# Regrouping the sixteen row blocks of h in a hybrid decoder block

## The chip, the core and the metric

The kernel runs on one core of one Trainium2 chip. The metric is the device time of one execution in microseconds (us), the median of several runs. A change of 0.2% is 1.6 us.

## The reference, cut to what matters

One decoder sub-layer for 256 tokens of width 2048, in float32. A conditioning vector `c` gives shift, scale and gate; `x` is normalised and modulated into `h`, and one wide product with `w_in` (2048 x 11824) feeds everything behind it.

```python
ada = c @ w_ada + b_ada
shift, scale, gate = jnp.split(ada, 3, axis=-1)
h = rms_norm(x, g_pre) * (1.0 + scale[:, None, :]) + shift[:, None, :]
proj = h @ w_in
(qa, kc, vc, ks, vs, kw, vw, ga, za, qb, kb, vb, zb, ma, mb) = jnp.split(proj, IN_SPLITS, axis=-1)
...
oa = nsa_attention(qa, kc, vc, ks, vs, kw, vw, ga, ...)
ya = (oa * jax.nn.silu(za)) @ w_br_a
ob = dilated_mixture(partial_rope(qb), partial_rope(kb), vb)
yb = (ob * jax.nn.silu(zb)) @ w_br_b
merged = jax.nn.sigmoid(ma) * ya + jax.nn.sigmoid(mb) * yb
out = merged @ w_out
return x + gate[:, None, :] * rms_norm(out, g_post)
```

A row block below is 128 of the 2048 rows of `w_in`, and with it 128 of the columns of `h`; there are sixteen, 0 to 15. A row block of `h` can be made only when the 2 x 128 entries of `ada` that belong to it (its shift and its scale) have been summed over all of `c`, and for one block that takes two 1 MB pieces of `w_ada`.

## The kernel before, in words

**Products.** The columns of `w_in` are cut into panels of 512 (one of 256, `kw`, and one of 304, `vw`): kc, ks, two of qa, kw, vw, two each of qb, kb, vb, za, zb, and four each of ma and mb. A weight item (`w_item`, L440) is one load of up to 1024 columns by 128 rows of float32: two row blocks of one panel, or one row block of two neighbouring panels. Each item is loaded into one of six `raw` buffers (`dma`, L552), split by ScalarE into a rounded part `wH` (L583) and by VectorE into the rest `wL` (L584), each with three buffers; then TensorE multiplies it for both halves of the 256 tokens: wH with the rounded h (L648), wH with the rest of h (L650), wL with the rounded h (L653). Two row blocks of a 512-column panel are 12 such products. For za and zb the operands are swapped (L638, L640, L643), and the same item is 24 products of half the size.

**Passes.** Since h comes block by block, the panels are gone over in passes (`PASSES`, L27): block 0; blocks 1 and 2; blocks 3 to 6; blocks 7 to 15. At the end of its pass, a panel's partial sum is moved out of PSUM and added to what lies in SBUF (`evac`, L727: L748 on ScalarE, L750 and L752 on VectorE). Between the third and the fourth pass lies a stretch called `FILL`: there only za and zb go on, with blocks 7 to 12. Their sums stay in the eight PSUM banks from the third pass to the end of `FILL`, where the four panels finish one after the other. The four panels of ma start late: their blocks 0 to 2 are put at the end of the second pass, and their sums stay in PSUM until they have had their blocks of the third.

**h.** The pieces of `w_ada` are ada items. Each is a load of 1 MB (128 x 2048, one row block of one half of `ada`), which VectorE multiplies by `c` and sums in one instruction (L595). Of the first twelve, six go into a tile `early`; the others, and all later ones, share a ring of two buffers, `raw_ada` (`RAW_ADA` = 2). `PIECES` (L32) says which blocks of h are made together and in which pass their ada items run; `spread` (L453) deals them out between the weight items of the pass, over the first `frac` of them, after `skip` items. After the last ada item of a group, `make_h` (L302) makes the group: two small VectorE instructions (L305, L306), one ScalarE instruction for each block (L311), the rounding on ScalarE (L318), and the rest on VectorE (L320). A product that needs a block of a group waits for that whole group (`need`, L695).

**Order.** The list of items is the order in which the program is written. Loads are issued seven items ahead (`LOADS`) from the one queue of SyncE, which works in order: a load that waits for its buffer holds up all loads behind it. Splits and ada sums are written three items ahead (`AHEAD`). On each engine the tile framework then fixes an order when the program is built, by place in the list and by when it expects operands. TensorE takes the items in the order of the list. Attention and the rest (`side_main`) are written as steps, one step for each weight item of the last pass.

Of the kernel before, what the change touches and what calls it, by code (L numbers as in the profile page):

```python
# [23 lines left out]
THETA = 500000.0  # L24
C_QA, C_KC, C_KS, C_KW, C_ZA, C_QB, C_KB, C_VB, C_ZB, C_MA, C_MB = (
    0, 1024, 1536, 2048, 2608, 3632, 4656, 5680, 6704, 7728, 9776)
PASSES = ((0, 1), (1, 3), (3, 7), (7, 16))  # L27
FILL = (7, 13)
KEPT = ("za", "zb")
LATER = ("ma",)  # L30
SECOND = ("kc0", "qa0", "kw0", "vw0", "qa512", "qb0", "ks0", "qb512", "kb0", "kb512", "vb0", "vb512")
PIECES = (((1, 3),), ((3, 7),), ((7, 10), (10, 13)), ((13, 16),))  # L32
AHEAD = 3
RAW = 6
RAW_ADA = 2
# [21 lines left out]
def _build(ctx, tc, d_in, out):  # L57
# [216 lines left out]
    xH = big.tile([128, KT, S], F32R, name="xH")  # L274
# [17 lines left out]
    xL, xT = Parts(), {}  # L292
# [123 lines left out]
    items = []  # L416
# [23 lines left out]
    def w_item(w, kt0, nk, c0, jobs):  # L440
        it = Item()
        it.kind, it.kt0, it.nk, it.jobs, it.whole = "w", kt0, nk, jobs, False
        it.n = sum(j.n for j in jobs)
        it.src = weights(w, kt0, nk, c0, it.n)
        return it

    def w_part(w, a, b, c0, job):
        return [w_item(w, kt, min(2, b - kt), c0, [job]) for kt in range(a, b, 2)]

    def w_job(w, a, b, c0, n, srcT, key):  # L450
        return w_part(w, a, b, c0, Job(n, a, b, srcT, key))

    def spread(ws, others, frac, skip=0):  # L453
        res, j = [], 0
        for i, w in enumerate(ws):
            res.append(w)
            want = max(0, min(len(others), math.ceil(len(others) * (i + 1 - skip) / (frac * (len(ws) - skip)))))
            res.extend(others[j:want])
            j = want
        res.extend(others[j:])  # L460
        return res
# [15 lines left out]
    def pieces(i):  # L477
        return [it for p in PIECES[i] for it in ada_items(p)]

    a, b = PASSES[0]  # L480
    ws = []
    soon = [p for p in partial if p[0] not in LATER]
# [9 lines left out]
    for n, it in enumerate(ws):  # L492
        items.append(it)
        if n in SUM_BEHIND:
# [3 lines left out]
    a, b = PASSES[1]  # L498
# [1 line left out]
    ws += [it for p in seconds for it in w_job("w_in", a, b, p[1], p[2], (xH, xL), ("proj", 1, 0, p))]  # L500
    pass1 = len(items)
    late_jobs = [(p, Job(p[2], 0, PASSES[2][1], (xH, xL), ("proj", 0, 0, p))) for p in partial if p[0] in LATER]
    ws += [it for p, job in late_jobs for it in w_part("w_in", 0, b, p[1], job)]
    items += spread(ws, pieces(1), 0.8, 3)
    a, b = PASSES[2]
    kept_jobs = [(p, Job(p[2], a, FILL[1], (xH, xL), ("proj", 2, 0, p))) for p in soon if p[0] in KEPT]
    ws = [it for p, job in late_jobs for it in w_part("w_in", a, b, p[1], job)]
    ws += [it for p in soon if p[0] not in KEPT
           for it in w_job("w_in", a, b, p[1], p[2], (xH, xL), ("proj", 2, 0, p))]
    ws += [it for p, job in kept_jobs for it in w_part("w_in", a, b, p[1], job)]  # L510
    items += spread(ws, pieces(2), 0.9, 2)
    ws = [it for p, job in kept_jobs for it in w_part("w_in", *FILL, p[1], job)]
    items += spread(ws, pieces(3), 0.8)
    a, b = PASSES[3]
    pass3 = len(items)
    for n, p in enumerate(panels):
        a_ = FILL[1] if p[0] in KEPT else 0 if p[0] == "mb" else a
        ws, cks = w_job("w_in", a_, b, p[1], p[2], (xH, xL), ("proj", 3, 1, p)), []
        if n in (3, 4):
            for q in range(4):  # L520
                it = Item()
                it.kind, it.which, it.q, it.nk, it.n = "ck", n - 3, q, 4, 256
                it.src = weights(("w_ck1", "w_cv1")[n - 3], 4 * q, 4, 0, 256)
                cks.append(it)
        items += spread(ws, cks, 0.8)
# [3 lines left out]
    ws = []  # L529
# [4 lines left out]
    for half in range(2):  # L534
        for kt in range(KT):
            it = Item()
# [747 lines left out]
    n = len(items)  # L1284
# [93 lines left out]
```

## Time and profile before

| | before |
|---|---|
| median of 3 runs | 802.17 us (802.14 to 802.52) |
| the profiled execution's own time | 802.07 us |
| its span, first to last instruction | 800.1 us |
| TensorE matmuls busy, of the span | 783.9 us |
| VectorE busy | 652.8 us |
| ScalarE busy | 446.4 us |
| moved by DMA | 195.32 MB, 244 GB/s on average |

A row of a profile names the line, the engine (PE is TensorE, PEld its weight loads, DVE is VectorE, ACT is ScalarE, SP is SyncE with its queue SPq), the operation, the tiles written and read, and a count; then the busy time and the mean length of one in ns. TensorE's matmuls overlap: one takes longer than the distance to the next, so a busy share near 100% does not say that it runs as fast as it can. How many start in a stretch does.

### The profile page before, as it was taken

How to read it: one execution, taken by the hardware profiler on the slowest of the kernel's cores; microseconds unless marked ns; L12 is line 12 of the kernel's file. 1: busy time of each engine (PE TensorE's matmuls, PEld its weight loads, DVE VectorE, ACT ScalarE, POOL GpSimd, SP SyncE). 2: the span in 40 equal slices, each digit the busy share in tenths (PEclk: the TensorE clock that was granted, in tenths of full speed). 3: DMA queues.
4: the chain of work that ended last, by engine and by line, in shares of the span. 5: the costliest groups of instructions: out<-in, count | busy, mean ns of one | idle time of the engine just before them, and what ended most of it. 6: DMA issues, size and time to landing. Idle time of an engine off the chain costs nothing.

```text
span 800.1 us, 11652 instructions
## 1 busy us (share of the span) xinstructions
PE 783.9 (98%) x4151; PEld 664.5 (83%) x4151; DVE 652.8 (82%) x962; ACT 446.4 (56%) x734; POOL 78.4 (10%) x125
## 2 busy tenths in 40 slices
PE   8999999999999999999999999999999999999995
PEld 6797788889998889787889888888888888888884
DVE  7879888998887979899889995778797888866554
ACT  4876554434344655677779885455644434445451
POOL 1000000000000045153322120011000000000000
PEclk9999999999999999999999999999999999999998
DMA  9999598897886477543433446457778889876633
GB/s 348 419 423 379 194 421 326 323 371 271 324 313 199 154 244 252 171 154 122 132 120 119 165 134 203 145 186 236 236 261 309 297 297 334 301 266 198 191 122 105
DMA packets 52928, 195.32 MB, mean 244 GB/s; under 512 B 6131, under 2 KB 7174, under 8 KB 48392
## 3 DMA queue, kind: packets, MB, share of 16 engines
q1 hardware_dynamic: 52272, 191.30, 68.2%
q10 hardware_dynamic: 600, 3.29, 1.1%
q8 instruction: 32, 0.52, 0.3%
q14 instruction: 24, 0.20, 0.1%
HBM read 192.47 MB, written 2.10 MB: 243 GB/s over the span
## 4 chain that ended last, share of the span: by engine, by line
PE 86%; DVE 7%; ACT 3%; DMA 2%; issue 2%; SPq 0%; DVEq 0%; ACTq 0%
PE mm L653 23%; PE mm L648 23%; PE mm L650 23%; PE mm L643 3%; PE mm L638 3%; PE mm L640 3%; DVE wL L584 2%; DMA raw<-in_w_first_dram 1%; PE pt_ps L1029 1%; PE sA L993 1%; PE mm L626 1%; ACT wH L583 1%; DMA xT<-in_xT_dram 1%; PE pvb_ps L1170 1%; PE sB L1160 1%
## 5 line engine op out<-in xcount | busy, mean ns | idle before, releaser
L583 ACT ACTIVATE wH<-raw 128x1024 fp32r<-128x1024 f32 (+2 forms) x273 | 272.0, 1000 | 259.2 <-PE mm L650 197.7
L584 DVE TENSOR_TENSOR wL<-raw,wH 128x1024 fp32r<-128x1024 f32 (+2 forms) x273 | 318.3, 1173 | 106.6 <-ACT wH L583 104.5
L648 PE MATMUL mm<-wH,xH 128*128 128x512 f32 (+2 forms) x636 | 244.2, 385 | 0.1
L650 PE MATMUL mm<-wH,xL 128*128 128x512 f32 (+2 forms) x636 | 241.7, 382 | 0.0
L653 PE MATMUL mm<-wL,xH 128*128 128x512 f32 (+2 forms) x636 | 197.5, 383 | 2.4 <-DVE wL L584 2.2
L653 PEld LDWEIGHTS mm<-wL,xH 128*128 128x128 f32 x636 | 116.8, 188 | 27.9 <-DVE wL L584 6.1
L648 PEld LDWEIGHTS mm<-wH,xH 128*128 128x128 f32 x636 | 119.6, 188 | 21.5 <-ACT wH L583 1.0
L650 PEld LDWEIGHTS mm<-wH,xL 128*128 128x128 f32 x636 | 119.6, 188 | 21.0 <-issue 0.2
L640 PE MATMUL mm<-xL,wH 128*128 128x256 f32 x240 | 62.3, 280 | 0.0
L638 PE MATMUL mm<-xH,wH 128*128 128x256 f32 x240 | 62.2, 281 | 0.0
L595 DVE SCALAR_TENSOR_TENSOR raw_ada<-raw_ada,ST 128x2048 f32<-128x2048 f32 x24 | 54.8, 2285 | 0.6 <-DMA raw_ada<-in_w_ss_dram 0.6
L648 PE MATMUL mm<-wH,yH 128*128 128x512 f32 x128 | 50.4, 394 | 0.0
L648 PE MATMUL mm<-wH,mH 128*128 128x512 f32 x128 | 50.0, 391 | 0.0
L650 PE MATMUL mm<-wH,mL 128*128 128x512 f32 x128 | 49.9, 390 | 0.0
L650 PE MATMUL mm<-wH,yL 128*128 128x512 f32 x128 | 49.9, 390 | 0.0
L643 PE MATMUL mm<-xH,wL 128*128 128x256 f32 x240 | 49.0, 280 | 0.0
L640 PEld LDWEIGHTS mm<-xL,wH 128*128 128x128 f32 x240 | 45.0, 188 | 0.0
L638 PEld LDWEIGHTS mm<-xH,wH 128*128 128x128 f32 x240 | 44.9, 188 | 0.1
L599 DVE SCALAR_TENSOR_TENSOR gacc<-raw,vT,gacc 128x1024 f32<-128x1024 f32 x32 | 41.1, 1283 | 0.0
L653 PE MATMUL mm<-wL,mH 128*128 128x512 f32 x128 | 39.8, 389 | 0.0
L653 PE MATMUL mm<-wL,yH 128*128 128x512 f32 x128 | 39.4, 389 | 0.0
L643 PEld LDWEIGHTS mm<-xH,wL 128*128 128x128 f32 x240 | 37.1, 188 | 0.1
(304 smaller groups left out, 962.4 us busy)
## 6 DMA issues: line engine op xcount, KB each, us to landing
raw<-in_weights_dram SPq DMA_DIRECT2D x237, 512.0 KB, 4.6
raw_ada<-in_w_ss_dram SPq DMA_DIRECT2D x24, 1024.0 KB, 6.9
raw<-in_w_gate_dram SPq DMA_DIRECT2D x32, 512.0 KB, 5.2
raw<-in_weights_dram SPq DMA_DIRECT2D x29, 256.0 KB, 3.1
early<-in_w_ss_dram SPq DMA_DIRECT2D x6, 1024.0 KB, 9.7
raw<-in_weights_dram SPq DMA_DIRECT2D x7, 304.0 KB, 2.9
xs<-in_x_dram SPq DMA_DIRECT2D x2, 1024.0 KB, 6.0
xr<-in_x_dram ACTq DMA_DIRECT2D x2, 1024.0 KB, 6.5
```

The lines of the kernel that those rows point to most:

```text
L583: highest[0] = A.activation(H, raw, AF.Copy)
L584: lowest[0] = V.tensor_tensor(L, raw, H.bitcast(F32), op=OP.subtract)
L595: V.scalar_tensor_tensor(r, r, 1.0, cB.rearrange("p a n -> p (a n)"), op0=OP.mult, op1=OP.mult, accum_out=sums[:, it.half, it.kt0:it.kt0 + 1])
L599: V.scalar_tensor_tensor(acc, raw[:, 0, :], cT[:, it.kt0:it.kt0 + 1], acc, op0=OP.mult, op1=OP.add)
L626: T.matmul(job.ps[t][:, b * S:(b + 1) * S], lhsT=it.raw[:, j, c0:c0 + 128], rhs=hj, start=(first and j == 0 and b == 0), stop=(last and j ...
L638: T.matmul(ps, lhsT=it.H[:, j, bs], rhs=sH[:, it.kt0 + j, :], start=(first and j == 0 and b == 0), stop=False, skip_group_check=True)
L640: T.matmul(ps, lhsT=it.H[:, j, bs], rhs=sL[:, it.kt0 + j, :], start=False, stop=False, skip_group_check=True)
L643: T.matmul(ps, lhsT=it.L[:, j, bs], rhs=sH[:, it.kt0 + j, :], start=False, stop=(last and j == it.nk - 1), skip_group_check=True)
L648: T.matmul(ps, lhsT=sH[:, it.kt0 + j, ts], rhs=it.H[:, j, cs], start=(first and j == 0), stop=False, skip_group_check=t in job.seeded)
L650: T.matmul(ps, lhsT=sL[:, it.kt0 + j, ts], rhs=it.H[:, j, cs], start=False, stop=False, skip_group_check=t in job.seeded)
L653: T.matmul(ps, lhsT=sH[:, it.kt0 + j, ts], rhs=it.L[:, j, cs], start=False, stop=(last and j == it.nk - 1), skip_group_check=t in job.seeded)
L993: T.matmul(o, lhsT=QT[:, u.t, h // 2, h % 2, :], rhs=KTt[:, hl, :, 0:128] if u.t == 0 else KTt[:, hl, u.br, :], start=(hl == 0), stop=(hl ...
```

## The change

The groups in which h is made become 1, 2, 3, 2, 3, 3 and 2 blocks; they were 1, 2, 4, 3, 3 and 3. The third pass covers blocks 3 to 5 and the fourth blocks 6 to 15. `FILL` becomes two rounds: za and zb first all take blocks 6 to 9, then all take blocks 10 to 13, and only 14 and 15 are left to them in the fourth pass. Each round carries the ada items of one group.

A pass of three blocks would leave a single block, a load of half the size, at the end of each panel. A new function, `w_pairs`, puts the third blocks of two neighbouring panels into one item of full size; two panels then are three items. The blocks 0 to 2 of ma in the second pass are treated the same way. The sums of a pair of panels therefore end together. In the second pass the ada items start after one weight item (`skip` 1) instead of after three.

```diff
-PASSES = ((0, 1), (1, 3), (3, 7), (7, 16))
-FILL = (7, 13)
+PASSES = ((0, 1), (1, 3), (3, 6), (6, 16))
+FILL = ((6, 10), (10, 14))
-PIECES = (((1, 3),), ((3, 7),), ((7, 10), (10, 13)), ((13, 16),))
+PIECES = (((1, 3),), ((3, 6),), ((6, 8), (8, 11)), ((11, 14),), ((14, 16),))
...
+    def w_pairs(w, a, b, jobs):
+        res = []
+        for (p, f), (q, g) in zip(jobs[::2], jobs[1::2]):
+            even = b - (b - a) % 2
+            res += w_part(w, a, even, p[1], f) + w_part(w, a, even, q[1], g)
+            if even < b:
+                res.append(w_item(w, even, 1, p[1], [f, g]))
+        return res
...
-    ws += [it for p, job in late_jobs for it in w_part("w_in", 0, b, p[1], job)]
-    items += spread(ws, pieces(1), 0.8, 3)
+    ws += w_pairs("w_in", 0, b, late_jobs)
+    items += spread(ws, pieces(1), 0.8, 1)
     a, b = PASSES[2]
-    kept_jobs = [(p, Job(p[2], a, FILL[1], (xH, xL), ("proj", 2, 0, p))) for p in soon if p[0] in KEPT]
-    ws = [it for p, job in late_jobs for it in w_part("w_in", a, b, p[1], job)]
-    ws += [it for p in soon if p[0] not in KEPT
-           for it in w_job("w_in", a, b, p[1], p[2], (xH, xL), ("proj", 2, 0, p))]
-    ws += [it for p, job in kept_jobs for it in w_part("w_in", a, b, p[1], job)]
-    items += spread(ws, pieces(2), 0.9, 2)
-    ws = [it for p, job in kept_jobs for it in w_part("w_in", *FILL, p[1], job)]
-    items += spread(ws, pieces(3), 0.8)
+    kept_jobs = [(p, Job(p[2], a, FILL[-1][1], (xH, xL), ("proj", 2, 0, p))) for p in soon if p[0] in KEPT]
+    others = [(p, Job(p[2], a, b, (xH, xL), ("proj", 2, 0, p))) for p in soon if p[0] not in KEPT]
+    items += spread(w_pairs("w_in", a, b, late_jobs + others + kept_jobs), pieces(2), 0.9, 2)
+    for n, (a, b) in enumerate(FILL):
+        ws = [it for p, job in kept_jobs for it in w_part("w_in", a, b, p[1], job)]
+        items += spread(ws, pieces(3 + n), 0.8)
     a, b = PASSES[3]
...
-        a_ = FILL[1] if p[0] in KEPT else 0 if p[0] == "mb" else a
+        a_ = FILL[-1][1] if p[0] in KEPT else 0 if p[0] == "mb" else a
```

## The prediction

> **What bounds the kernel now.** I read the head of the page first, then busy time by stretches, then who waited for whom.
>
> ```profile
> span 800.1 us, 11652 instructions
> PE 783.9 (98%) x4151; PEld 664.5 (83%) x4151; DVE 652.8 (82%) x962; ACT 446.4 (56%) x734; POOL 78.4 (10%) x125
> PE 86%; DVE 7%; ACT 3%; DMA 2%; issue 2%; SPq 0%; DVEq 0%; ACTq 0%
> ```
>
> TensorE is the bound, and the change takes no product away: every panel still meets every row block once. So only time in which TensorE is held up can be won or lost. The last line is the chain of waits: 7% of it is VectorE. The stretches show where.
>
> ```profile
> core 0: us, PE busy (x) PEld busy (x) DVE busy (x) ACT busy (x) POOL busy (x), PEclk, DMA share, GB/s
> 16.00:41.00 25.00, 23.84 (x102) 18.03 (x101) 19.93 (x24) 19.98 (x36) 0.00 (x0) 1.00 1.02 418
> 62.00:92.00 30.00, 28.11 (x117) 21.31 (x117) 29.20 (x36) 16.30 (x24) 0.00 (x0) 1.00 0.72 278
> 156.00:176.00 20.00, 20.00 (x90) 16.54 (x90) 20.00 (x23) 7.44 (x7) 0.00 (x0) 1.00 0.99 381
> 204.00:238.00 34.00, 34.00 (x289) 33.90 (x288) 29.27 (x31) 14.76 (x16) 0.00 (x0) 1.00 0.87 316
> 300.00:415.00 115.00, 113.73 (x631) 94.98 (x630) 102.04 (x195) 77.62 (x182) 42.67 (x59) 1.00 0.48 159
> 415.00:455.00 40.00, 39.07 (x283) 35.99 (x282) 38.28 (x77) 35.52 (x86) 8.56 (x7) 1.00 0.44 139
> ...
> PEld mm L653 <- DVE wL L584: 3.9, 5, 1.3
> PE mm L653 <- DVE wL L584: 1.7, 3, 0.8
> ...
> PEld mm L653 <- DVE wL L584: 0.4, 2, 0.3
> ```
>
> The counts in brackets are matmuls. In 156:176, in the third pass, 90 overlap the 20 us; I take two as reaching over an edge, so 88 start, one every 0.227 us. In 62:92 (second pass, the same 512-column products) 117 overlap, 115 start, and at that pace they need 115 x 0.227 = 26.1 us of the 30. **So 3.9 us are lost there.** The two waits behind the stretches are those of 57:93: TensorE waits for wL from VectorE, which was busy 29.20 of 30. The last line is the only wait of this kind in 99:242, the third pass and `FILL`: 0.4 us, though VectorE was busy 20.00 of 20.00 in 156:176. TensorE there keeps pace because the three wL buffers let VectorE run ahead. In 204:238 it starts about 287 half-size products in 34 us: 0.1185 each. Later, TensorE's idle time is 1.27 us in 300:415 and 0.93 in 415:455.
>
> **The prices.** These are VectorE's rows in `FILL`, and groups of the whole span.
>
> ```profile
> 201.65 2.28 DVE L595 SCALAR_TENSOR_TENSOR raw_ada<-raw_ada,ST 128x2048 f32<-128x2048 f32 x1
> 203.86 1.22 DVE L584 TENSOR_TENSOR wL<-raw,wH 128x1024 fp32r<-128x1024 f32 x1
> ...
> 223.68 0.69 DVE L750 TENSOR_TENSOR ZA<-mm,ZA 128x512 f32<-128x512 f32 x1 [1.58 <-PE mm L643]
> 224.28 2.28 DVE L595 SCALAR_TENSOR_TENSOR raw_ada<-raw_ada,ST 128x2048 f32<-128x2048 f32 x1
> 226.49 0.08 DVE L595 DVE_READ_ACCUMULATOR raw_ada<-raw_ada,ST 128x1 f32 x1
> 226.49 0.69 DVE L750 TENSOR_TENSOR ZA<-mm,ZA 128x512 f32<-128x512 f32 x1
> 227.10 2.35 DVE L584 TENSOR_TENSOR wL<-raw,wH 128x1024 fp32r<-128x1024 f32 x2
> 229.36 2.29 DVE L595 SCALAR_TENSOR_TENSOR raw_ada<-raw_ada,ST 128x2048 f32<-128x2048 f32 x1
> ...
> L583 ACT ACTIVATE wH<-raw 128x1024 fp32r<-128x1024 f32 x234 | 247.8, 1060 | 238.9 <-PE mm L650 183.1 <-PE mm L640 25.5 <-issue 11.4
> L311 ACT ACTIVATE ST<-xT,AB 128x256 f32<-128x256 f32 x13 | 6.8, 591 | 5.8 <-DVE AB L306 5.8
> L318 ACT ACTIVATE xH<-ST 128x768 fp32r<-128x768 f32 (+2 forms) x5 | 4.2, 834 | 0.0
> L320 DVE TENSOR_TENSOR xL<-ST,xH 128x768 fp32r<-128x768 f32 (+2 forms) x5 | 4.8, 953 | 0.0
> ```
>
> From start to start, an ada sum costs VectorE 2.21 us, a full wL 1.13 (two in 2.26), an eviction of one half of a panel 0.61. A group of three blocks costs it about 2 (L320 and as much again for scaling x and the small ones). An item costs TensorE 12 x 0.227 = 2.72 us, or 24 x 0.1185 = 2.84 for za and zb. The lead: wL's buffer is free two items before its own (5.4 us), the splits take 1.06 and 1.22, and the first wL product comes four products into the item (0.9); 5.4 - 2.3 + 0.9 = 4.0 us.
>
> **Second pass.** Its group shrinks from four blocks to three, from eight ada items to six, dealt out one after about every three weight items instead of every two.
>
> ```profile
> L595 DVE SCALAR_TENSOR_TENSOR raw_ada<-raw_ada,ST 128x2048 f32<-128x2048 f32 x3 | 6.8, 2283 | 0.0
> L595 DVE SCALAR_TENSOR_TENSOR early<-early,ST 128x2048 f32<-128x2048 f32 x2 | 4.6, 2282 | 0.0
> ```
>
> These are the sums in 62:92, five. Counting along the new list, three fall between the same weight items. VectorE has 29.2 - 2 x 2.21 = 24.8 us of work for 26.1 of products, 95%; the third pass runs at 100% without loss. I keep 0.4 us for uneven places: **-3.5 us**. Bounds: -3.9, and -2.0 if the evictions, which come in clumps here, go on holding it up. The first two sums move two items forward in SyncE's queue, past two weight loads each, while DMA is full (418 GB/s): 1.05 MB, 2.5 us of delay, hidden by items loaded seven ahead, about 20 us. If that cover were gone, it would cost those 2.5 us.
>
> **Third pass.** The twelve panels other than ma, za and zb amount to 11.1 of full width. Before: 11.1 x 4 blocks x 6 x 0.227 = 60.5 us on TensorE; on VectorE 22.2 splits 25.1, 22.2 evictions 13.5, 8.4 ada sums (12 over 34.2 items) 18.6, one group 2: 59.2, 98%. After: 45.3 us on TensorE; 16.65 splits 18.8, evictions 13.5, 7.1 sums (10 over 25.2 items) 15.7, one group 2: 50.0. VectorE is 4.7 us over. ma goes before and needs little of VectorE, so it enters with its lead of 4.0: **+0.7 us**. Bounds: 0, as the framework can put a sum behind a split that TensorE wants, and 4.7 without any lead. za and zb follow with 17 us of products against 6 splits, one sum, four evictions and a group, 13.4: the lead comes back. A pair of panels evicts four halves at once (2.4 us), but the next pair has its four banks from the pair before, 8.2 us earlier: nothing.
>
> **The two rounds.** Each is 8 items, 22.7 us. VectorE has in the first 8 splits (9.0), six sums (13.3) and a group (2): 1.6 over; in the second 9.0, four sums 8.8, eight evictions 4.9 and about 1.5 for two blocks: 1.5 over. Together 3.1, within the lead. What may not be hidden is the ring.
>
> ```profile
> 203.97 0.33 SPq L564 DMA_DIRECT2D raw_ada<-in_w_ss_dram  x1
> 204.71 0.33 SPq L564 DMA_DIRECT2D raw<-in_weights_dram  x1
> ...
> raw<-in_weights_dram SPq DMA_DIRECT2D x237, 512.0 KB, 4.6
> raw_ada<-in_w_ss_dram SPq DMA_DIRECT2D x24, 1024.0 KB, 6.9
> ...
> early<-in_w_ss_dram SPq DMA_DIRECT2D x6, 1024.0 KB, 9.7
> ```
>
> An ada load goes out as soon as the sum two before it has ended (203.97, behind the sum of 201.65 that ended at 203.9), takes 6.9 us, and weight loads queue behind it. The eviction at 223.68 waited for the first half of `FILL`'s sixth item, so `FILL` began 5.5 x 2.84 earlier, at 208.0, and its first sum at 6.3 us before that. With the same start, and time 0 at the round's first product: the second item's buffers are free at -2.8 and its splits done at -0.6 (1.06 and 1.13), so the second sum, behind them, ends at 1.6; the fourth's load lands at 8.5 and its sum ends at 10.7, the sixth's lands at 17.6 and ends at 19.8; three L311, L318 and L320 take 3.9 with the small ones: h of blocks 11 to 13 stands at 23.7. The first item of the second round needs it at 22.7. That is the wait which the change adds; behind it on TensorE stands everything, za's and zb's evictions and the fourth pass's banks included. **+1.0 us.** The seventh weight load, behind the sixth ada load, is 0.4 late within that. Bounds: 0 if an ada load takes the 4.6 us of the smaller ones (the chain then ends before 20); at 9.7 us each the group stands at 29.3, +6.6.
>
> **Fourth pass.** All panels now have five full items where they had four and a half-size one. Attention's steps come one per item, so each has 2.72 us of products beside it instead of 2.45: I take -0.3 of the 2.2 idle us above. za and zb lose an item each, four steps fewer, and these stand later: bounds -1.5 and +1.0.
>
> Sum: -3.5 + 0.7 + 1.0 - 0.3 = -2.1 us on the profiled 802.07 (span 800.1 and 2.0 around it), which is 0.1 under the median: **800.1 us**.
>
> **Rivals.** First, the ring decides (slower): the first round's ada loads take 9.7 instead of 6.9 us, and its end comes 6.6 us late: 802.2 - 3.5 + 0.7 + 6.6 - 0.3 = 805.7. It breaks even at loads of about 7.9. For it: six sums in 22.7 us, before in 9.6 items of 2.84, 27.3; with eight weight loads of 0.52 MB and six of 1.05 the round moves 10.5 MB. Against: two of the six are loaded before, and the rest, 8.4 MB, needs 20.1 us at the 418 GB/s of the first stretch. The Trainium skill, page "DMA: Bandwidth & Descriptors", section "Bandwidth", holds that for transfers from HBM the HBM side, about 358 GB/s for a core, binds rather than the fabric's 435: by it the 10.5 MB take 29.3 us, 6.6 over the round. The trace disagrees, with 418 GB/s over 25 us and 381 over 20. Second, VectorE decides in the third pass (no change or slower): no lead is left, +4.7 for +0.7, 804.1. For it: 20.00 of 20.00 busy already. Against: 0.4 us of waits there. Third, the second pass does not gain, as evictions were the cause: -1.5 and the rest as forecast, 802.1. Fourth, nothing of the third pass and the rounds shows and the fourth gains its 1.5: -3.9 - 1.5 = 796.8.
>
> **How the numbers follow.** What a measurement can tell from no change is 0.2%, 1.6 us. The forecast, 798.8 to 801.5, has 42%, three quarters of it more than 1.6 us faster; the fourth rival 17%, all faster; the third 15%, same; the second 12%, a quarter same; the first 14%, slower. Faster 0.42 x 0.75 + 0.17 = 0.49, same 0.105 + 0.15 + 0.03 = 0.28, slower 0.23. Leaving out half of the fastest and half of the slowest case, the range is 797.4 to 804.9.
>
> **What would show it.** In the second pass, waits of TensorE for wL near 0.5 us instead of 5.6, and a product every 0.227 us. In the third, VectorE without idle time and waits for wL under 1 us. At the start of the second round, TensorE waiting about 1 us for L320. Wrong would be: waits for wL in the second pass above 2 us (third rival), several us of them in the third (second), or a hole over 3 us between the rounds (first).

## The result, and the profile after

The kernel after takes 809.48 us (median of six runs, 808.13 to 812.29), the kernel before beside it 802.26; the ratio is 1.0094 [1.0076, 1.0112]. It is 7.2 us slower where 2.1 less were forecast. The profiled execution took 809.08 us, its span is 807.3.

First the head of the page of after, and the busy time by stretches (columns as in the prediction).

```profile
span 807.3 us, 11591 instructions
PE 783.7 (97%) x4151; PEld 664.3 (82%) x4151; DVE 654.0 (81%) x954; ACT 442.9 (55%) x723; POOL 72.7 (9%) x125
```

```profile
62.00:92.00 30.00, 30.00 (x137) 24.86 (x136) 28.30 (x35) 20.05 (x28) 0.00 (x0) 1.00 0.77 270
162.00:180.50 18.50, 18.50 (x152) 17.96 (x151) 18.19 (x21) 8.84 (x11) 0.00 (x0) 1.00 0.68 252
180.50:203.00 22.50, 19.02 (x151) 17.80 (x149) 18.06 (x18) 6.05 (x8) 0.00 (x0) 1.00 0.96 355
203.00:228.00 25.00, 23.08 (x192) 22.50 (x193) 23.03 (x27) 12.42 (x16) 0.00 (x0) 1.00 0.98 383
```

TensorE's work is the same (783.7 us, 4151 products). The second pass has what was forecast: 30.00 of 30 busy, 137 products where there were 117, and in 57:93 no wait of TensorE for wL is left. The time went in the two rounds, 180 to 233 us: TensorE stands idle for 3.5 of 22.5 us, then for 1.9 of 25, and the transfers run at 0.96 to 0.98 of their time, directly behind a stretch in which they ran at 0.68.

To put numbers on stages I took the distance from each product's start to the next one's, subtracted the usual distance for that kind of product in the same run (its median), and added up what is above it. This "lost" time holds for all runs below.

| us lost | za and zb at the start of the second pass (41 to 54) | rest of second, third pass | za, zb of third pass and FILL or rounds | fourth pass, up to its za |
|---|---|---|---|---|
| before | 0.2 | 4.0 | 0.2 | 9.4 |
| after | 1.8 | 0.7 | 8.2 | 10.4 |

So 3.3 us were won in the second pass, 1.6 lost at its start, 8.0 in the rounds, 1.0 in the fourth pass and 0.5 elsewhere: 7.8 in all, for 7.2 more of span, as some products of the rounds ran at a faster pace (see the end). Who waited for whom in the rounds (180:228, the first four rows), and what the queue of SyncE did:

```profile
ACT wH L590 <- DMA raw<-in_weights_dram: 24.2, 8, 4.8
DVE raw_ada L602 <- DMA raw_ada<-in_w_ss_dram: 4.2, 3, 2.3
PEld mm L645 <- ACT wH L590: 3.8, 3, 2.6
PEld mm L650 <- DVE wL L591: 3.4, 6, 1.5
```

```profile
170.97 0.33 SPq L571 DMA_DIRECT2D raw<-in_weights_dram  x1
179.86 0.33 SPq L571 DMA_DIRECT2D raw_ada<-in_w_ss_dram  x1
180.28 0.38 SPq L571 DMA_DIRECT2D raw<-in_weights_dram  x1
183.20 0.33 SPq L571 DMA_DIRECT2D raw_ada<-in_w_ss_dram  x1
183.62 0.38 SPq L571 DMA_DIRECT2D raw<-in_weights_dram  x1
187.20 0.33 SPq L571 DMA_DIRECT2D raw_ada<-in_w_ss_dram  x1
187.62 0.86 SPq L571 DMA_DIRECT2D raw<-in_weights_dram  x1
192.09 0.33 SPq L571 DMA_DIRECT2D raw_ada<-in_w_ss_dram  x1
...
```

From 171 to 179.9 the queue issues nothing: the next ada load waits for the sum that frees its ring buffer, and all weight loads stand behind it. Then it issues one weight load behind each ada load, every 3 to 5 us, up to 192; in 162:203 it waits 17.6 us in all for ada sums. ScalarE gets its weights late (24.2 us of waiting for loads), and so TensorE gets its wH late. ScalarE's rows for the fifth to seventh items of the first round, each split right behind its load:

```profile
191.00 1.06 ACT L590 ACTIVATE wH<-raw 128x1024 fp32r<-128x1024 f32 x1 [3.80 <-DMA raw<-in_weights_dram]
194.66 1.06 ACT L590 ACTIVATE wH<-raw 128x1024 fp32r<-128x1024 f32 x1 [2.61 <-DMA raw<-in_weights_dram]
200.51 1.06 ACT L590 ACTIVATE wH<-raw 128x1024 fp32r<-128x1024 f32 x1 [4.79 <-DMA raw<-in_weights_dram]
```

TensorE waited 0.6, 0.4 and 2.6 us for these three.

### The profile page after: what moved, and what is told of

It reads as the page before. It is cut to its first block, busy times and chain, and to the rows that moved or that the text cites. A ratio compares the mean times of both kernels' runs of the same rounds, so it can differ in the third digit from the quotient of the medians.

```text
span 807.3 us, 11591 instructions
## 1 busy us (share of the span) xinstructions
PE 783.7 (97%) x4151; PEld 664.3 (82%) x4151; DVE 654.0 (81%) x954; ACT 442.9 (55%) x723; POOL 72.7 (9%) x125
## 4 chain that ended last, share of the span: by engine, by line
PE 51%; DVE 3%; ACT 1%; issue 1%; DVEq 0%; ACTq 0%
PE mm L660 15%; PE mm L655 15%; PE mm L657 15%; PE pt_ps L1036 1%; DVE wL L591 1%; PE sA L1000 1%; PE pvb_ps L1177 1%; PE sB L1167 1%; PE ot_ps L1058 1%; PE ot_ps L1060 1%; PE m_ps L1235 0%; PE b_ps L1152 0%; PE oc_ps L1131 0%; ACT P L1015 0%; ACT wH L590 0%
## 5 line engine op out<-in xcount | busy, mean ns | idle before, releaser
L660 PE MATMUL mm<-wL,xH 128*128 128x512 f32 (+2 forms) x636 | 195.2, 382 | 0.7 <-DVE wL L591 0.5
L650 PE MATMUL mm<-xH,wL 128*128 128x256 f32 x240 | 47.3, 283 | 2.3 <-DVE wL L591 2.1
```

What stands on the lines that cost most here:

```text
L650: T.matmul(ps, lhsT=it.L[:, j, bs], rhs=sH[:, it.kt0 + j, :], start=False, stop=(last and j == it.nk - 1), skip_group_check=True)
L660: T.matmul(ps, lhsT=sH[:, it.kt0 + j, ts], rhs=it.L[:, j, cs], start=False, stop=(last and j == it.nk - 1), skip_group_check=t in job.seeded)
```

## The experiments

Times are medians; each ratio is to the kernel before, run on the same chip beside it. The lost columns are those of the profiled run, which lies off the median by more than 0.9 us in three cases: e2 (819.9), e5 (802.38) and e15 (801.14). In e6 the small products have a shorter usual distance (113 ns, see the end) than they have at the start of the second pass; that is why 2.2 us count as lost there.

| run | us | ratio | lost: start | rest of second, third | rounds or FILL | fourth pass |
|---|---|---|---|---|---|---|
| e3 short loads | 807.19 | 1.0063 [1.0048, 1.0079] | 1.8 | 0.7 | 4.5 | 10.4 |
| e4 short sums | 808.46 | 1.0076 [1.0059, 1.0092] | 1.8 | 0.7 | 6.6 | 10.5 |
| e6 both short | 800.53 | 0.9985 [0.9976, 0.9994] | 2.2 | 0.6 | 0.7 | 10.5 |
| e2 GpSimd's queue | 817.14 | 1.0186 [1.0151, 1.0220] | 1.8 | 0.6 | 17.3 | 10.4 |
| e7 skip 3, ring of three | 821.16 | 1.0237 [1.0223, 1.0250] | 0.2 | 0.1 | 4.3 | 10.4 |
| e11 skip 3, seeded | 807.09 | 1.0056 [1.0041, 1.0072] | 0.2 | 1.0 | 6.5 | 10.5 |
| e1 skip 3 | 809.50 | 1.0086 [1.0071, 1.0101] | 0.2 | 1.0 | 8.8 | 10.5 |
| e8 before, skip 1 | 803.97 | 1.0025 [1.0015, 1.0036] | 1.8 | 4.3 | 0.2 | 9.5 |
| e12 no pairs | 808.58 | 1.0077 [1.0063, 1.0090] | 1.8 | 0.9 | 7.1 | 9.9 |
| e5 second pass only | 803.35 | 1.0011 [1.0003, 1.0020] | 0.2 | 3.4 | 0.7 | 9.4 |
| e9 the same, seeded | 803.44 | 1.0020 [1.0011, 1.0029] | 0.2 | 5.5 | 1.1 | 9.4 |
| e10 before, seeded | 802.48 | 1.0000 [0.9991, 1.0008] | 0.2 | 4.2 | 0.2 | 9.4 |
| e14 e5, scaling on GpSimd | 804.54 | 1.0026 [1.0015, 1.0037] | 0.2 | 5.6 | 0.7 | 9.4 |
| e15 e13, scaling on GpSimd | 803.10 | 1.0007 [0.9997, 1.0017] | 0.6 | 2.0 | 2.8 | 9.3 |
| e16 before, scaling on GpSimd | 803.04 | 1.0009 [0.9999, 1.0018] | 0.2 | 5.0 | 0.2 | 9.2 |
| e13 e5, dealt wider | 801.06 | 0.9983 [0.9974, 0.9993] | 0.2 | 0.7 | 2.1 | 9.3 |
| e18 before, dealt wider | 802.12 | 0.9996 [0.9987, 1.0005] | 0.2 | 3.9 | 0.2 | 9.4 |
| e17 e13, FILL wider too | 800.27 | 0.9972 [0.9961, 0.9982] | 0.2 | 0.6 | 0.9 | 9.8 |

### What loses the time in the rounds

**Loads cut (e3).** The last ten ada items load a quarter; the sum still reads 2048 columns, in two instructions.

```diff
-        DMA.dma_start(it.raw, it.src)
+        if it.kind == "ada" and it.at >= 20:
+            DMA.dma_start(it.raw[:, :512], it.src[:, :512])
+        else:
+            DMA.dma_start(it.raw, it.src)
...
```

> The changed kernel with the ten ada loads of the rounds cut to a quarter (512 of 2048 columns); VectorE still works through 2048 columns, in two instructions of 1536 and 512. The output leaves out the other three quarters of those ada sums. Theories Q and B (the loads are the limit, by the ring and the queue or by bandwidth): under 1.5 us lost in the rounds, 801.5 to 803 us. Theory V: still 8 us lost there, 809.

**Sums cut (e4).** The same ten items load all and sum a quarter (`r[:, :512]`, `cB[:, :512]`).

> The changed kernel with the ten ada sums of the rounds over 512 of the 2048 columns; the loads stay whole. The output leaves out three quarters of those sums. VectorE is relieved of 1.6 us for each, 16 us in all. Theory V: under 1.5 us lost in the rounds, 801.5 to 803 us. Theory Q: each step of the ring, some 9 us of load and sum, is shorter by 1.6, so about half of the 8 us stays: 805 to 806. Theory B: at least 6 us stay, over 807.

**Both cut (e6).**

> The kernel after, with the ada items of the rounds (the last ten) cut to a quarter in both: 512 of their 2048 columns are loaded and 512 are summed, so ada of those blocks is wrong in value; the order and number of items stay. Shorter loads alone took 3.7 us from the 8.2 that TensorE loses in the rounds, shorter sums alone 1.6. Theory D+V, that transfers and VectorE are each over their capacity there and that relieving one leaves the other: with both short, the rounds lose under 1.5 us, total 809.5 - 7 = 802.5 (801.5 to 804). Rival O, that the fixed order of the engines (ScalarE's scaling of a new group in front of the next split) holds TensorE by itself: 3 to 4 us stay, at the start of the second round, total 805 to 806.5. Under both, the 1.0 us more of the fourth pass and the 1.6 us at the start of the second pass stay.

Neither alone is the cause: e3 came out between its theories, e4 in the range of theory B, and e6 lost under 1.5 us in the rounds, as D+V expected. The stretches of the rounds in e3, e4 and e6:

```profile
180.50:203.00 22.50, 22.50 (x193) 22.50 (x193) 22.37 (x33) 8.49 (x8) 0.00 (x0) 1.00 0.80 263
203.00:228.00 25.00, 23.09 (x180) 22.39 (x180) 23.29 (x39) 12.01 (x15) 0.00 (x0) 0.93 0.61 197
```

```profile
180.50:203.00 22.50, 21.25 (x174) 20.55 (x174) 11.72 (x20) 9.40 (x11) 0.00 (x0) 1.00 1.01 412
203.00:228.00 25.00, 22.05 (x181) 21.24 (x180) 16.74 (x27) 9.77 (x11) 0.00 (x0) 1.00 0.85 331
```

```profile
180.50:203.00 22.50, 22.50 (x201) 22.50 (x201) 17.33 (x33) 12.90 (x16) 0.00 (x0) 1.00 0.93 333
203.00:228.00 25.00, 25.00 (x203) 24.24 (x202) 19.37 (x38) 11.38 (x13) 0.20 (x1) 1.00 0.60 199
```

With short loads VectorE is the one that is full (22.37 of 22.5); it then reaches the second round late, where TensorE waits 1.9 us for a split that ScalarE has queued behind the new group of h, and 0.5 for the group itself; the clock then falls (see the end), which is about 1.5 of the 4.5 us. With short sums VectorE is half idle and the transfers are full (1.01, 412 GB/s) in the first stretch; most of the loss comes in the second, where they run at 0.85. With both short TensorE has no idle time in 47.5 us. So loads and sums each held TensorE up, and each hid the other: relieving one recovers 3.7, the other 1.6, both 7.5. (e6's 800.53 holds 2 us more than that, from a faster pace of the products, told at the end.) Rival O fell: with both cut, the engines' fixed order holds up next to nothing.

**Ada loads in a queue of their own (e2).**

```diff
-        DMA.dma_start(it.raw, it.src)
+        (G if it.kind == "ada" and it.at >= 20 else DMA).dma_start(it.raw, it.src)
```

> The changed kernel with the ten ada loads of the two rounds issued from GpSimd's queue instead of SyncE's. Nothing else moves; the ring still has two buffers and the same bytes are read. Theory Q (in the rounds the weight loads are late because they queue on SyncE behind ada loads that wait for a buffer of the ring): ScalarE's waits for weight loads in the rounds, 24 us now, fall under 6, and of the 8 us of product time lost there 1 to 3 remain, the wait for h of blocks 11 to 13: 802.5 to 804.5 us. Theory B (transfers as such are the limit, 355 to 383 GB/s at a share of 0.96 to 0.98): at least 6 of the 8 us remain, over 807. Theory V (VectorE is over-full in the rounds): no change, 809.

It went the wrong way, 817.14. Theory Q's condition held, as ScalarE's waits for weight loads are gone from 180:228; its time did not. Ada loads now share the transfers with weight loads: VectorE waited 10.2 us for ada loads there, and its order puts sums ahead of the splits that TensorE needs. TensorE waited 4.8 us for the group of blocks 11 to 13 (xL), 4.2 for wL and 3.3 for wH, and the clock was at half for 13.6 us, part of it in these waits. That the weight loads stand behind the ring is how the loss arrives; taken out of the queue, it arrives through h and VectorE.

**A third ring buffer (e7),** with the skip of three. `RAW_ADA` 2 to 3, and `RAW` 6 to 4 to make room.

> The kernel after with the skip of three, with three ring buffers for ada loads instead of two, and, to make room for the third, four raw weight buffers instead of six. In the kernel after the transfers were at 0.68 of their time in 162 to 180.5 and at 0.96 to 0.98 in the 47 us behind it; the first load of the first round that waits for the ring went out at 179.9, when the sum two before it had ended. Theory D, that the rounds lose because these transfers start too late: with a third buffer that load goes out about 13 us earlier, the rounds lose 3 to 5 us instead of 8.2, and with the 1.6 of the skip the total is 803 to 805. Rival V, that VectorE sets the rounds: the loads come earlier and the rounds still lose 7 to 8 us, total 807 to 808. A rival of its own is that four raw buffers bring waits for weight loads in the other passes; they would show as waits for wH from the transfers outside the rounds, and take back up to 4 us.

The total is 821.16, but the extra lies elsewhere: 9.2 us lost ahead of 46 us (4.1 in after) and 13.2 behind 620 (1.2), where four weight buffers are too few: far more than the 4 us that its rival allowed. In the rounds the loss fell to 4.3, as theory D said. Its stretches, to be read against those of after:

```profile
162.00:180.50 18.50, 18.46 (x138) 17.25 (x136) 17.91 (x23) 8.69 (x11) 0.00 (x0) 1.00 0.84 304
180.50:203.00 22.50, 21.88 (x182) 21.39 (x181) 21.51 (x22) 8.79 (x10) 0.00 (x0) 1.00 1.02 423
```

The loads begin earlier (0.84 for 0.68) and then run at 423 GB/s, so the 355 of after is not what the transfers can do: it is a ring whose loads wait for sums and whose sums wait for loads. The skip is not the reason: e1, with the same skip and two buffers, moved 374 there.

**Less for VectorE ahead of the rounds (e11).** The skip of three, and nine panels of the third pass and za and zb seeded: for the second half of the tokens ScalarE puts the sum so far into the bank and copies the result out, in place of VectorE's addition.

```diff
-          ("proj", 3, "kb"), ("proj", 3, "vb"), ("proj", 3, "za"), ("proj", 3, "zb"), ("proj", 3, "ma"))
+          ("proj", 2, "kc"), ("proj", 2, "qa"), ("proj", 2, "qb"), ("proj", 2, "kb"), ("proj", 2, "vb"),
+          ("proj", 2, "za"), ("proj", 2, "zb"), ("proj", 3, "kb"), ("proj", 3, "vb"), ("proj", 3, "za"), ("proj", 3, "zb"), ("proj", 3, "ma"))
...
-            if o.jobs[0].key[:2] in (("proj", 1), ("proj", 3)) and it.jobs[0].key[0] == "proj":
+            if o.jobs[0].key[:2] in (("proj", 1), ("proj", 2), ("proj", 3)) and it.jobs[0].key[0] == "proj":
```

> The kernel after with the skip of three, and with the third pass's panels seeded in the same way, za and zb included: the latter takes four of the eight evictions at the end of the second round off VectorE (2.4 us) and the others 5.5 us off its third pass, so that the ada sums of blocks 6 to 10 end earlier and the ring is free earlier for the first round. Theory D+V: transfers remain over what the rounds can carry, VectorE no longer is at the first round's start; the rounds lose 5 to 6.5 us instead of 8.2, total 809.5 - 1.6 - 2.5 = 805.4 (804 to 807). Rival D, that the transfers alone set the rounds once they begin late: 8 us stay, total 807 to 808. Rival V, that VectorE's arrears at the start of the first round set both: the loss falls under 4, total under 804.

The rounds lose 6.5 us, at the end of what D+V expected; the total, 807.09, is just above its range. Evictions are a small part.

### The forward move of the ada items

> The changed kernel with the ada items of the second pass starting after three weight items again instead of after one. Theory S (the first ada load now stands ahead of the loads of zb's weights, and ScalarE got an order in which the split of the third item of the second pass stands behind three evictions that wait for TensorE): the 2 us lost between 46 and 55 us go, the rest stays: about 807.4 us. Rival (that order is an accident of the forward move and comes back elsewhere, or the loss is a late transfer): 809 us or more, with the loss in the same place or a little later. Neither expects a change in the two rounds, some 8 us lost.

> The kernel before with one number changed: the ada items of the second pass start after one weight item instead of after three. The prediction priced this move at nothing, as items are loaded seven ahead. Theory S, that it costs 1.6 to 2 us, since ScalarE's fixed order puts the split of za's and zb's third item behind the evictions and seeds of the panels before, once its load stands later in the queue: TensorE waits for wH at about 46.5 us, the first stretch of the second pass loses 1.8 us instead of 0.2, total 803.8 to 804.2. Rival, the prediction's: no change, 802.2 plus or minus 0.4. A second rival: the two ada items more room behind them are worth something in the kernel before, whose second pass is short of VectorE, and the total is 0.5 to 1 us under 802.2.

In both only the skip differs, and the start of the second pass loses 0.2 with three and 1.8 with one, in all runs but e15 (0.6) and e6 (2.2, by its other usual distance). In the kernel before that is 1.6 us of total time, as theory S said. In e1 it does not show in the total, which came out where the rival had it: its rounds lost 0.6 more, with a drop of the clock in them (see the end), and its runs spread over 2 us. ScalarE's rows at that place, before and then e8:

```profile
38.51 2.06 ACT L583 ACTIVATE wH<-raw 128x1024 fp32r<-128x1024 f32 x2
42.98 0.60 ACT L748 ACTIVATE ZA<-mm 128x512 f32<-128x512 f32 x1 [2.42 <-PE mm L643]
```

```profile
38.64 1.04 ACT L583 ACTIVATE wH<-raw 128x1024 fp32r<-128x1024 f32 x1
43.12 0.60 ACT L748 ACTIVATE ZA<-mm 128x512 f32<-128x512 f32 x1 [3.44 <-PE mm L643]
...
46.34 0.60 ACT L671 ACTIVATE mm<-QA 128x512 f32<-128x512 f32 x1
46.88 1.04 ACT L583 ACTIVATE wH<-raw 128x1024 fp32r<-128x1024 f32 x1
```

Two splits stood ahead of the first eviction; with skip 1 only one does, and the second comes 7 us later, behind the evictions and the seeds. Its load had landed at 43.2 (issued at 33.4, 9.8 us): in time, and no longer awaited. TensorE waits 1.2 us for the split.

### The pairing

> The kernel after without the pairing: the third block of each panel is an item of its own with a load of half the size (256 KB), as in the kernel before, so that every panel of the third pass and of ma in the second has one full and one half-size item. The prediction priced the pairing at nothing by itself. Theory: the products are the same in number, and what changes are six more items in the second and third pass each with half-size splits; their fixed part is small (a half-size split takes ScalarE 0.63 against 1.06 us), VectorE's third pass grows by about 12 x 0.1 us and the lead in items is worth less in time; total 809.5 to 812. Rival, that pairing costs something (two panels end together and their four evictions come at once): without it the total falls by 1 us or more, to 808.5 or below.

808.58 lies between the two, and its interval overlaps that of after. Pairing is neither the cause nor a cure.

### The second pass alone

**e5** takes the kernel before and cuts only the second pass's group. Block 6 becomes a group of its own at the head of the third pass.

```diff
-PIECES = (((1, 3),), ((3, 7),), ((7, 10), (10, 13)), ((13, 16),))
+PIECES = (((1, 3),), ((3, 6),), ((6, 7), (7, 10), (10, 13)), ((13, 16),))
...
-    ws = [it for p, job in late_jobs for it in w_part("w_in", a, b, p[1], job)]
+    ws = [it for k in range(a, b, 2) for p, job in late_jobs for it in w_part("w_in", k, k + 2, p[1], job)]
```

> The kernel before, with only the group of the second pass cut: blocks 3 to 5 are made from six ada items in the second pass, and block 6 becomes a group of its own whose two ada items stand at the head of the third pass. For that the third pass takes blocks 3 and 4 of all four panels of ma first and then 5 and 6. FILL, the fourth pass, the pairing and the skip of three stay as in the kernel before. Theory 1, that the second pass gains what the prediction said and the loss all comes from what the change does behind it: the waits for wL in 57 to 93 fall from 5.6 us to about 1, VectorE's third pass has 59.2 + 4.4 + 1 = 64.6 us of work for 60.5 of products but a lead of 4.0 and the slack of za and zb behind it, so 0 to 1 us comes back there; total 802.2 - 3.3 + 0.5 = 799.4 (798.6 to 800.5), faster than both kernels. Rival, that a denser third pass gives the gain back as the denser rounds do: 4 us of new waits for wL or for loads in 99 to 185, total 802 to 804.

The second pass was won (30.00 busy of 30 in 62:92) and given back in the third, 2.0 us of it at one place. VectorE there:

```profile
150.63 1.22 DVE L584 TENSOR_TENSOR wL<-raw,wH 128x1024 fp32r<-128x1024 f32 x1
151.76 0.47 DVE L750 TENSOR_TENSOR VW<-mm,VW 128x304 f32<-128x304 f32 x1
152.15 0.95 DVE L593 TENSOR_TENSOR xT<-xT,rstdB 128x768 f32<-128x768 f32 x1
153.78 0.69 DVE L752 SCALAR_TENSOR_TENSOR QB<-mm,QB 128x512 f32<-128x512 f32 x1 [0.69 <-PE mm L653]
154.39 0.95 DVE L320 TENSOR_TENSOR xL<-ST,xH 128x768 fp32r<-128x768 f32 x1
155.26 2.29 DVE L595 SCALAR_TENSOR_TENSOR raw_ada<-raw_ada,ST 128x2048 f32<-128x2048 f32 x1
...
157.47 1.22 DVE L584 TENSOR_TENSOR wL<-raw,wH 128x1024 fp32r<-128x1024 f32 x1
```

From the end of one split to the start of the next lie 5.6 us, more than the 4.0 of lead that the prediction reckoned with. That more ada items had already used part of the lead is argued here; e13 below bears it out.

**Moving VectorE's work away (e9, e10, e14, e15, e16).** e9 is e5 with the nine seeded panels; e10 is before with them. e14 is e5 with the scaling of x on GpSimd from block 6 on, e15 has the wider dealing of e13 as well, e16 is before with that scaling.

```diff
-                    V.tensor_tensor(xn, xn, rstdB[:, None, :].to_broadcast([128, xn.shape[1], S]), op=OP.mult)
+                    (G if it.piece[0] >= 6 else V).tensor_tensor(xn, xn, rstdB[:, None, :].to_broadcast([128, xn.shape[1], S]), op=OP.mult)
```

> The kernel with only the second pass's group cut and block 6 on its own, and beside it nine panels of the third pass seeded: for their second half of the tokens ScalarE puts the sum so far into the PSUM bank before the products and copies the result out behind them, in place of VectorE's addition. That takes 9 x 0.61 = 5.5 us off VectorE between 110 and 170 us, and gives ScalarE, busy 8 to 12 of 20 there, 18 instructions of 0.59. Theory 1, that VectorE is the bound of both passes, so that the two ada sums moved out of the second pass cost in the third what they brought (3.9 against 3.1 lost): with VectorE relieved, the third pass loses under 0.5 us, total 802.3 - 3.3 = 799.0 (798.4 to 800.0), faster than both kernels. Rival, that the third pass waits for a load or for the fixed order of the sums and not for VectorE's time: the 2.0 us at about 156 stay, total 802 to 803. A second rival: seeds wait for the bank's eviction at the head of ScalarE's queue and hold up splits behind them; waits for wH appear in 110 to 170 and the total rises above 803.

> The kernel before with the same nine panels of the third pass seeded, and nothing else changed: the control for the run beside it. Theory 1: VectorE's third pass was full but held nobody up (0.4 us of waits), so 5.5 us less of work there bring 0 to 0.5 us, total 801.8 to 802.4, and the 3.9 us of the second pass stay lost. Rival: the seeds themselves bring something or cost something, total 1 us or more off 802.3 to either side.

> The kernel with only the second pass's group cut, and the scaling of x for the groups from block 6 on given to GpSimd, idle until then, in place of VectorE. It takes 0.95 us off the bunch of 5.3 us at each group of three blocks, and gives ScalarE nothing, other than the seeds, which put their own waits in front of the splits. Theory 1 (VectorE's time is the bound of the third pass, too): the wait at 156.5 falls from 2.0 to about 1.0 and the third pass loses 2 us in place of 3.1, total 801.2 to 802.0. Rival B (the bunch as such): the same number, as both say that 0.95 of the bunch goes; they part in the run beside it, where pace and bunch are both relieved. Rival G: GpSimd's work slows VectorE's beside it by more than it saves, or a group waits for GpSimd; total above 803.

> The kernel with only the second pass's group cut, with both reliefs: ada items over all of the third pass, and the scaling on GpSimd. If VectorE's time is all that gave the second pass's gain back, the third pass loses 0 to 1 us and the total is 799.3 to 800.8, faster than both kernels by more than 0.2%. If waits of more than 1.5 us remain in 99 to 185, what gives it back is the order fixed at build time, which falls differently with each list, and the total is 801.5 to 803.5.

> The control: the kernel before with the scaling of x from block 6 on given to GpSimd and nothing else changed. VectorE's time in its third pass held nobody up, so both theories expect 802.3 plus or minus 0.5; anything else would be the price or the gain of GpSimd's scaling by itself and comes off the two runs beside it.

None of them helped. The seeds made ScalarE the late one, in e9 at the same group:

```profile
155.06 0.60 ACT L749 ACTIVATE QB<-mm 128x512 f32<-128x512 f32 x1 [1.46 <-PE mm L654]
155.69 0.60 ACT L672 ACTIVATE mm<-VB 128x512 f32<-128x512 f32 x1
156.23 2.94 ACT L584 ACTIVATE wH<-raw 128x1024 fp32r<-128x1024 f32 x3
```

Three splits wait behind an eviction and a seed, and TensorE for 2.5 us; the clock then fell (see the end). On GpSimd the scaling of a group of three takes 2.31 us in the row below, against VectorE's 0.95. e14 and e15 got a new wait of 1.3 us for block 6 at 112 us, and e14's trace shows what made it, GpSimd's row first:

```profile
106.58 2.31 POOL L593 TENSOR_TENSOR xT<-xT,rstdB 128x768 f32<-128x768 f32 x1 [10.03 <-DMA xT<-in_xT_dram]
107.10 3.94 DVE L595 SCALAR_TENSOR_TENSOR raw_ada<-raw_ada,ST 128x2048 f32<-128x2048 f32 x1
```

The ada sum that VectorE begins while GpSimd scales takes 3.94 us in place of 2.29. It is the last of block 6's group, which is late by that much. It goes the same way in e15, where the split ahead of that group's end took 2.86 us at 109.05 in place of 1.23. In e14 the three groups of three cost VectorE 1.65, 1.46 and 1.24 us in this way and saved it 0.95 each, as the first half of rival G said. The controls are level (e10) or 0.7 slower (e16, with an interval that includes no change). The Trainium skill, page "Perfetto Trace Analysis", section "Optimizing Scalar/DVE Operations", says that work may be moved to ScalarE or GpSimd where VectorE is saturated; here neither paid, as ScalarE has splits of its own and GpSimd's work held up VectorE's.

**Dealing wider (e13, e18, e17).** e13 is e5 with the ada items over all of the third pass, e18 the same in before, e17 is e13 with those of `FILL` over all of it.

```diff
-    items += spread(ws, pieces(2), 0.9, 2)
+    items += spread(ws, pieces(2), 1.0, 2)
...
-    items += spread(ws, pieces(3), 0.8)
+    items += spread(ws, pieces(3), 1.0)
```

> The kernel with only the second pass's group cut, its fourteen ada items of the third pass dealt out over all of that pass instead of its first nine tenths, so one after 2.4 weight items instead of 2.1. Without it TensorE lost 2.0 us once, at 156.5, where VectorE had one group's scaling, an eviction, the group's rest and an ada sum (5.3 us) between two splits. Theory P, that VectorE's pace in the third pass decides (13 ada sums in 30 items instead of 12 over 34): one ninth fewer sums for each item leave it 0.1 us for each item more, the lead is not used up before the group, that wait falls under 0.7 us, total 800.5 to 801.5. Rival B, that the bunch at the group decides, whatever the pace: it moves with the group and still costs 1.5 to 2.5 us, total 802 to 803.5.

> The control for the wider dealing: the kernel before with its twelve ada items over all of the third pass instead of nine tenths, nothing else changed. If the gain of the wider dealing is only that it makes room for what the second pass gives up, there is nothing to gain here: 802.0 to 802.5, and perhaps 0.5 to 1.5 more for waits in FILL as the later groups' sums come into it. Rival: the wider dealing is a gain by itself, and the total falls to 801.5 or less; then the cut of the second pass's group is not what made the kernel beside it faster.

> The kernel with only the second pass's group cut and the ada items over all of the third pass (801.06, 1.2 us faster than before), and the six ada items of FILL over all of its twelve weight items instead of the first four fifths. Of its 3.3 us won in the second pass that kernel lost 1.9 again in FILL, in three waits of 0.5 us for wL at 217 to 227, where two sums of 2.2 us lie between neighbouring splits. Theory P, that pace is all: one sum for every two items instead of every 1.6, the three waits go, and the total is 799.3 to 800.3. Rival T, that FILL's transfers then end too late: the group of blocks 13 to 15 stands later at the start of the fourth pass, which waits 1 us or more for it; total 801 to 802.

e13 and e17 are faster than both kernels, e18 shows that the wider dealing alone is worth nothing. The bunch is still there in e13 (5.2 us between two splits, 155.7 to 160.9) and costs 0.2 us: theory P held, B fell. A bunch longer than the reckoned lead of 4.0 thus costs little where the lead ahead of it is whole. In FILL e13 waited 1.7 us in all for wL; in e17 these waits are mostly gone, without a wait for the last group. The rows are two stretches of e17:

```profile
62.00:92.00 30.00, 30.00 (x134) 24.69 (x133) 28.71 (x37) 18.96 (x27) 0.00 (x0) 1.00 0.76 259
185.00:242.00 57.00, 56.64 (x470) 55.84 (x469) 47.92 (x50) 25.44 (x28) 0.00 (x0) 1.00 0.82 312
```

## Why the prediction was wrong

**Second pass, -3.5: right,** -3.3 measured (4.0 to 0.7 lost, third pass included), for the reason given: the waits for wL are gone, and VectorE's evictions did not hold it up (third rival out).

**The forward move, priced at nothing: wrong, +1.6.** "Hidden by items loaded seven ahead" looked at the load, and of that it was true: the load landed 2.9 us later (42.8 in after, 39.9 in e1), before the product at 46.4 needed it. What came late was the split: ScalarE's order, fixed when the program is built, no longer had it ahead of the evictions.

**Third pass, +0.7: about nothing,** 0.4 us of waits for wL as before. Rival two is out.

**The two rounds, +1.0: wrong, +8.0.** This step failed. The sums of the ring were forecast fairly well, though the first began at -2.6 and not at -6.3: counted from the round's first product (180.2), the fourth sum ended at 11.9 (forecast 10.7), the sixth at 21.4 (19.8). The group behind them stood at 27.7 (23.7): 6.3 us behind the last sum in place of 3.9. TensorE did not wait for the group, for the round itself ran to 27.8 in place of 22.7 us. With weight loads in time, and all else equal, it would have waited 5.0 us for it, an estimate from these times; so the wait that the term was made of was mis-sized too, and hidden. What TensorE did wait for is in the sentence "The seventh weight load, behind the sixth ada load, is 0.4 late within that": the seventh came 2.6 us late by itself, behind 0.6 and 0.4 for the two ahead of it. It went out at 192.5, behind the sixth ada load, and took 7.9 us; I had priced a weight load at the 4.6 us of the whole span. The loads issued in 180:203 of after, and in 204:238 (`FILL`) of before:

```profile
raw_ada<-in_w_ss_dram SPq DMA_DIRECT2D x6, 1024.0 KB, 7.7
raw<-in_weights_dram SPq DMA_DIRECT2D x9, 512.0 KB, 8.6
```

```profile
raw<-in_weights_dram SPq DMA_DIRECT2D x13, 512.0 KB, 6.3
raw_ada<-in_w_ss_dram SPq DMA_DIRECT2D x4, 1024.0 KB, 5.5
```

The median of the whole span comes mostly from stretches with half the traffic; `FILL`'s own 6.3 was there to be read. And "together 3.1, within the lead" spent the same 4.0 us of lead in the third pass, in the first round, in the second, and on late loads. e3 shows what VectorE's part is without any late load: 4.5 us lost, of which 2.4 are two waits and about 1.5 the clock behind them.

**Fourth pass, -0.3: wrong in sign, +1.0,** the upper bound given, in all runs with the new grouping but e12 (+0.5), whatever was done to the rounds. Two waits at 296 and 309 us, for VectorE's part of the compression's hidden layer, amount to 1.1 us:

```profile
PE hidT_ps L894 <- DVE gu L889: 1.1, 2, 0.6
```

In before the same products waited 0.2; the other places of the pass about cancel. What moved these two was not tried.

**The rivals.** The first had the right place, the ring in the first round, and a price (6.6 us) that the 5.2 us lost in that round come near. It made h late, by way of ada loads of 9.7 us: h was 5.0 us late, but with ada loads of 7.7, and the weight loads held the round up just as long, so that no wait for h shows. The rate of 358 GB/s that the Trainium skill gives (page "DMA: Bandwidth & Descriptors", section "Bandwidth") matches the 355 of 180.5:203 only by chance; with the sums cut the same stretch moved 412, with a third buffer 423.

## What to carry to other kernels

Price a transfer from the stretch that is as dense as the one you are about to make, not from the whole span. A lead between engines is one store: spend it once in the sum, not once per stage. Work that is moved out of a held-up stretch pays only where the receiving stretch takes it at a pace that leaves the lead alone; here the same cut lost 1 us or won 2.1, by how widely the moved items were dealt.

## What the runs showed of the hardware that I had not expected

**The clock fell behind a wait.** In e3 TensorE waited 1.9 us at 203.7 and then 0.5; the granted clock fell to half for 3.4 us. Its stretches:

```profile
197.00:203.70 6.70, 6.70 (x59) 6.70 (x58) 6.70 (x11) 2.66 (x4) 0.00 (x0) 1.00 0.86 289
203.70:207.00 3.30, 1.58 (x10) 1.17 (x10) 3.07 (x6) 2.73 (x5) 0.00 (x0) 0.95 0.84 279
207.00:210.30 3.30, 3.11 (x15) 2.82 (x15) 3.30 (x6) 0.00 (x0) 0.00 (x0) 0.54 0.53 166
```

15 products in 3.3 us, where 28 fit: 1.5 us more for a wait of 2.4. The same happened in e1 (203), e9 (159), e2 (197, and 10.2 us from 214 on) and e7 (19, 682 and 705), but not behind the 2.6 us of after's profiled run, so a wait's length alone does not decide; what does was not settled. The Trainium skill, page "Perfetto Trace Analysis", section "Matmul Optimizations", says that TensorE's power follows its use and that products should run back to back; these rows agree, and after's wait of 2.6 us shows that not every gap is paid for. In e3 a wait of 2.4 us cost 3.9 in all. It may be why after's runs spread over 4 us: the one of 812.29 had a mean clock of 0.994, the one of 808.13 of 0.998.

**The small products have two paces.** The swapped products of za and zb start every 118 ns in nearly all stretches, but every 113 in some, at the same granted clock: in e6 from 171 to 224 us, which is worth 2 us there, and in after behind the waits at 214 and 224. In e6 no wait stands ahead of the switch, only one distance of 150 ns. What switches them was not found.

**GpSimd's work stopped VectorE's.** In e14, e15 and e16 an ada sum or a split that VectorE began while GpSimd scaled x ended about as much behind GpSimd's end as it usually takes: the sum above ended at 111.04, 2.15 us behind 108.89. Even an instruction of 0.17 us (L305) took 1.69, in e15 at 196.52. Two evictions out of PSUM that began under GpSimd's scaling (e15, 153.91 and 154.30) kept their length of 0.47 and 0.46.
